# One decoder layer on one Trainium2 core: scores moved beside the values of the head in front, 512-column matmuls first in each such place

## The chip, the core and the metric

The kernel runs on one core of one Trainium2 chip. The metric is the device time of one execution in microseconds (us), the median over the runs shown. An engine is one of PE (TensorE, matmuls; its weight loads are listed apart as PEld), DVE (VectorE), ACT (ScalarE), POOL (GpSimd, here mostly a queue that issues DMAs) and SP (the queue that issues the weight loads from memory). Each engine works through its own list of instructions in the order in which the built program has them; semaphores make one engine wait for another.

## What is computed

One layer of a decoder over 256 tokens and 2048 features: sixteen heads of latent attention beside a short gated convolution, both projected, gated, added, and projected once more. Cut to what matters here:

```python
h = _rmsnorm(x, pre_norm_g)
proj = einsum('bsd,de->bse', h, w_in)          # q_a, c_kv, k_rope, z_mla, c_in, b_gate, c_gate, z_conv, g_mla, g_conv
q  = einsum('bsr,re->bse', _rmsnorm(q_a, q_a_norm_g), w_q_b)     # 16 heads x (128 + 64)
kv = einsum('bsr,re->bse', _rmsnorm(c_kv, kv_a_norm_g), w_kv_b)  # 16 heads x (128 keys + 128 values)
sc = (einsum('bqhd,bkhd->bhqk', q_nope, k_nope) + einsum('bqhr,bkr->bhqk', q_rope, k_rope)) * scale
p  = softmax(where(mask, sc, -inf))
attn = einsum('bhqk,bkhd->bqhd', p, v) * silu(z_mla)
y_mla = attn @ w_o_mla
y_conv = (b_gate * conv(c_gate * c_in) * silu(z_conv)) @ w_o_conv
out = (sigmoid(g_mla) * y_mla + sigmoid(g_conv) * y_conv) @ w_out
x = x + _rmsnorm(out, post_norm_g)
```

## The kernel before

**Numbers in two parts.** Every matmul operand is split into a high part (the value rounded to the matmul's format) and a low part (the rest), and a product is made of three matmuls (`product`, lines 227 to 232). A weight half of 128 x 1024 is split by `split_act` (lines 242 to 249): ACT copies it into a `whi` buffer (line 243), DVE subtracts to give `wlo` (line 244). There are five buffers of each kind; a buffer is free when PE has done its last matmul with it. `ahead` and `take` (lines 202 to 222) load three weight units ahead and split one unit ahead. The same two lines also split other things: `pt` is the split of a head's turned probabilities, `qn_hi`/`qn_lo`, `kn` and `qr` are the splits of queries and keys.

**The middle part** (lines 779 to 858; roughly from 70 to 590 us of the span) is a loop over the sixteen heads h, with v, at = divmod(h, 4). It mixes two kinds of work on PE. The big kind is `channels(h, i)`, i = 0 to 3, and, at every fourth head, `gates(v, i)`: a quarter each, 24 matmuls of 512 columns into two PSUM banks (`quarter`, lines 670 to 676). Between the quarters stand the small steps of attention:

- `group_a(g)`: queries qn and keys kn of two heads. `narrow` and `halves` (lines 234 to 240, 546 to 555) do 8 matmuls of 512 columns for qn, then 8 of 256, evict both banks (`whole`, lines 390 to 394: ACT copies one half out, DVE adds the other) and split; then the same for kn.
- `group_r(g)`: the rotary queries qr, 4 matmuls of 512 and 4 of 256 columns.
- `group_v(v)`: the values of four heads, 24 matmuls of 512 columns.
- `scores(h)`: 8 matmuls, seven of 256 columns and one of 128, then the softmax on DVE and ACT; the exponentials are at line 630. `turned` transposes p on DVE into `via` and POOL sends it to memory in four DMAs (go, line 326); come (line 330) brings it back as p.
- `turn(p)`: splits it into pt (lines 642 to 647); its two instructions are kept in program order.
- `values(h, pt)`: one matmul of 512 columns, then 256, 128 and 256, then `whole` and a product with the gates.

In the version before, the score of head h stands before `channels(h, 0)` (line 812); pt of head h-1 is made after `channels(h, 1)`; values of head h-1 follow `channels(h, 2)` (line 832), with group_a or group_r behind them (`made`, lines 118 to 122: qr at even heads, qn and kn at odd ones, each for the next pair). Where at = 0 and v > 0, the four quarters of the gates come first; pt is made after the second of them and values(h-1) and group_v stand after the third (lines 794 to 799).

**What sets the order.** PE's order is written out: every matmul is kept in program order. On ACT and DVE most instructions are placed by the scheduler that builds the program; a few are kept in order. ACT needs a table in place for some functions: sigmoids (lines 686, 721) and exponentials (line 630) use different ones, and the build puts a table load where the function changes.

Of the kernel before, what the change touches and what calls it, by code (L numbers as in the profile page):

```python
# [12 lines left out]
F32R = mybir.dt.float32r  # L13
# [5 lines left out]
P = 128  # L19
# [63 lines left out]
def tile_layer(ctx: ExitStack, tc: tile.TileContext, xw, w0, xb, x, pos, pvec, post_g, wc, wz, wcv, wkr, wqk, wqr, wv, cwr, wsq, out):  # L83
    nc = tc.nc

    def matmul(*a, **kw):

        return tc.keep_in_program_order(nc.tensor.matmul(*a, **kw))  # L88
# [113 lines left out]
    def ahead(i, raw=3, split=1):  # L202
        while done["raw"] < min(i + raw, len(plan)):
            load_raw(done["raw"])
            done["raw"] += 1
        while done["split"] < min(i + 1 + split, len(plan)):
            while done["raw"] <= done["split"]:
                load_raw(done["raw"])
                done["raw"] += 1
            split_unit(done["split"])  # L210
            done["split"] += 1

    def take(i):
        ahead(i)
        parts = splits.pop(i)

        def piece(j, n):
            o = j * n
            h, o = o // HALF, o % HALF
            return parts[h][0][:, o : o + n], parts[h][1][:, o : o + n]  # L220

        return piece
# [8 lines left out]
        matmul(ps, ah, bl, start=False, stop=False)  # L231
        matmul(ps, al, bh, start=False, stop=last)

    def halves(blocks):


        for ps, w, both, first, _ in blocks:
            matmul(ps[:, :], w[0], both, start=first, stop=False)
        for ps, w, both, _, last in blocks:
            matmul(ps[:, :S], w[1], both[:, :S], start=False, stop=last)  # L240

    def split_act(hi, lo, src, keep=False, later=False):
        a = nc.scalar.activation(hi, src, AF.Copy)  # L243
        b = nc.vector.tensor_tensor(lo, src, hi.bitcast(F32), op=ALU.subtract)  # L244
        if keep:

            tc.keep_in_program_order(a)
        if keep or later:
            tc.keep_in_program_order(b)
# [56 lines left out]
    def temp(name, shape=(P, S), dt=F32, bufs=2, tag=None):  # L306

        tag, n = tag or name.rstrip("0123456789_"), shape[-1]
        if n % LINE == 0:
            return bp.tile(list(shape), dt, name=name, tag=tag, bufs=bufs)  # L310
        return bp.tile([P, -(-n // LINE) * LINE], dt, name=name, tag=tag, bufs=bufs)[:, :n]
# [78 lines left out]
    def whole(dst, ps):  # L390

        t = temp("half")
        nc.scalar.activation(t[:, :], ps[:, S:], AF.Copy)
        nc.vector.tensor_tensor(dst, ps[:, :S], t[:, :], op=ALU.add)
# [146 lines left out]
    def pair(name, shape, bufs=1):  # L541
        return [temp(f"{name}_{n}", shape, F32R, bufs, tag=f"{name}_{n}") for n in ("hi", "lo")]

    groups = {}

    def narrow(names, w, j, src, **kw):
        pss = [bank(n, **kw) for n in names]
        halves([
            (ps, w((j + i) * KR + k, P), src[:, k, :], k == 0, k == KR - 1)
            for i, ps in enumerate(pss) for k in range(KR)  # L550
        ])
        for ps in pss:
            f = temp("f")
            whole(f[:, :], ps)
            yield f

    def group_a(g):

        qn, kn = pair("qn", (P, HG, S)), temp("kn", (P, 2, HG, S), F32R, 1)
        w = take(u_grp["a", g])  # L560
        for n, src, hi, lo in (("qn", qa, qn[0], qn[1]), ("kn", ckv, kn[:, 0], kn[:, 1])):
            fs = narrow([f"{n}{g}_{j}" for j in range(HG)], w, HG * (n == "kn"), src)
            if g == 0 and n == "qn":

                fs = list(fs)
                ahead(u_grp["v", 0])
            for j, f in enumerate(fs):
                split_act(hi[:, j, :], lo[:, j, :], f[:, :])
        groups["a", g] = qn, kn

    def group_r(g):

        qr = temp("qr", (P, HG, S), F32R)

        kw = {} if g else {"tag": "cv", "bufs": 2}
        (f,) = narrow([f"qr{g}"], take(u_grp["r", g]), 0, qa, **kw)
        rope(f[:, :], f[:, :])
        for j in range(HG):

            own, other = (slice(DR * i, DR * i + DR) for i in (j, 1 - j))  # L580
            split_act(qr[own, j, :], qr[other, j, :], f[own, :], g == 0)
        groups["r", g] = qr

    def group_v(v):

        vv = pair("vv", (P, NT, HV * DV))
        w = take(u_grp["v", v])
        for t in range(NT):
            ps = bank(f"vv{v}_{t}")
            for k in range(KR):  # L590
                c = [ckv[:, k, o + t * P : o + (t + 1) * P] for o in (0, S)]
                product(ps[:, :], c, w(k, HV * DV), k == 0, k == KR - 1)
            split_act(vv[0][:, t, :], vv[1][:, t, :], ps[:, :], v == 0)
        groups["v", v] = vv

    def make(i, j):
        {"a": group_a, "r": group_r, "v": group_v}[i](j)

    def scores(h):

# [48 lines left out]
    def values(h, pt):  # L649
        vv = groups["v", h // HV]  # L650
        j = h % HV
        o = bank(f"o{h}", tag="o", bufs=1)
        vs = slice(j * DV, (j + 1) * DV)
        both = o[:, :].rearrange("p (i q) -> p i q", i=2)
        mm = matmul
        mm(both, vv[0][:, 0, vs], pt[:, :, :S], start=True, stop=False)
        mm(o[:, :S], vv[1][:, 0, vs], pt[:, 0, :S], start=False, stop=False)
        mm(o[:, P:S], vv[1][:, 1, vs], pt[:, 0, S:], start=False, stop=False)
        mm(both[:, :, P:], vv[0][:, 1, vs], pt[:, :, S:], start=False, stop=True)

        at = at_t[:, h // HV, :, :].rearrange("p t (i k x) -> p t i k x", i=4, k=HV)[:, :, :, j, :]
        f = temp("f")
        whole(f[:, :], o)
        nc.vector.tensor_tensor(at, f[:, :].rearrange("p (t i x) -> p t i x", t=NT, i=4), at, op=ALU.mult)
# [36 lines left out]
    def channels(h, i):  # L701

        if i == 0:
            cv_ps["now"] = [bank(f"cv{h}_{t}", tag="cv", bufs=2) for t in range(NT)]
        quarter(cv_ps["now"], take(u_head[h][i]), i)
        if i == 3:
            channels_done(*divmod(h, 4))
# [71 lines left out]
    for h in range(H):  # L779
        v, at = divmod(h, HV)  # L780

        if at == 0:
            for i in range(4):
                gates(v, i)
                if v == 0 and i == 0:
                    ckv_come()
                elif v == 0 and i == 1:
                    next(table_parts)
                    key_rope()
                elif v == 0 and i == 2:  # L790
                    latent_split("qa", qa, "q_g")
                elif v and i == 0:
                    arrive()
                elif v and i == 1:
                    pt = turn(ps_by_head.pop(h - 1))
                    next(tap)
                elif v and i == 2:
                    values(h - 1, pt)
                    make("v", v)
            if v:  # L800
                next(tap)
            else:
                latent_split("ckv", ckv, "kv_g")
            gates_done(v)
        if h == 0:

            ahead(u_grp["r", 0])
            for i in first:
                make(*i)
            channels(h, 0)  # L810
        if h < H - 1:
            score(h)
        if h:
            channels(h, 0)
        if at == 0:
            coming.append(gates_turn(v, 0))
        channels(h, 1)
        if at == 0:
            arrive()
            coming.append(gates_turn(v, 1))  # L820
        else:
            pt = turn(ps_by_head.pop(h - 1))
        if h == H - 2:
            score(h + 1)

        if at == 2 or h == H - 1:
            next(tap)
        if at and h < H - 1:
            arrive()
        channels(h, 2)  # L830
        if at:
            values(h - 1, pt)
        else:
            arrive()
            if v:
                coming.append(channels_join(v - 1, 0))
        for i in made[h]:
            make(*i)
        if h == H - 1:
            pt = turn(ps_by_head.pop(h))  # L840
        channels(h, 3)
        if at == 2 or h == H - 1:
            next(tap)
        while coming and h < H - 1:
            arrive()
        if h == H - 1:
            values(h, pt)
        if at == 3:
            coming.append(channels_join(v, 1))
        if at == 1:  # L850
            tap = taps(v, 1)
            next(tap)
        elif at == 3 and h + 1 < H or h == H - 2:
            tap = taps(v, 0)
            next(tap)
# [280 lines left out]
```

## Time and profile before

| | |
|---|---|
| median of 3 runs | 1035.66 us (1035.56 to 1035.92) |
| the profiled execution | 1034.93 us, of it the span from its first to its last instruction 1033.2 us |
| PE busy | 1026.7 us, 99% of the span, 4680 matmuls |
| DVE busy | 682.9 us, 66% |
| ACT busy | 526.7 us, 51% |
| granted TensorE clock | 0.999 |
| largest weight loads | 80 + 64 + 16 loads of 1 MB (raw from wsq, wcv and wz) |

The groups of instructions are read as line, engine, operation, tile written <- tiles read, count | busy us, mean ns of one | idle time before them and what ended it. A row of the timeline is: start in us, length in us, engine, line, operation, tiles, shape, count and, in brackets, the idle time before it with what ended it. The stated ends of matmuls are modelled and overlap the next one, so the time a matmul takes in a stream is read from start to start.

### The profile page before, as it was taken

The page shows a single profiled execution, that of the slowest core. Times are in us where ns is not written, and L with a number is a line of the kernel's source. Part 1 is how long each engine was busy: PE and PEld are TensorE (multiplying, and loading weights), DVE is VectorE, ACT ScalarE, POOL GpSimd, SP SyncE. Part 2 cuts the span into 40 slices and gives each one's busy share as a digit, 9 for nine tenths or more (in the row PEclk, how much of TensorE's full clock was granted, in tenths as well). Part 3 has the DMA queues.
Part 4 walks back from the last instruction along what each step waited for, and adds up shares of the span by engine and source line. Part 5 has one row for each costly group of instructions (what it writes and reads, how often), then busy time and mean ns, then how long its engine had stood idle before and what let it go on. Part 6 is the DMA issues. An engine that isn't in the chain of part 4 may idle for free.

```text
span 1033.2 us, 12728 instructions
## 1 busy us (share of the span) xinstructions
PE 1026.7 (99%) x4680; PEld 855.0 (83%) x4680; DVE 682.9 (66%) x957; ACT 526.7 (51%) x734; POOL 179.8 (17%) x344
## 2 busy tenths in 40 slices
PE   9999999999999999999999999999999999999997
PEld 7888888888888888888888888888888888888886
DVE  7588777777787777767767785564455455455562
ACT  7766545555455454564555565344434444443551
POOL 4640421104201142112413120020010001002000
PEclk9999999999999999999999999999999999999999
DMA  9775766568565775856766765565565556558642
GB/s 359 281 252 215 267 236 215 204 220 284 194 254 186 232 283 187 278 179 244 264 236 225 258 222 201 204 223 190 199 217 208 189 202 242 180 189 336 230 167 81
DMA packets 44670, 233.25 MB, mean 226 GB/s; under 512 B 7968, under 2 KB 10656, under 8 KB 21696
## 3 DMA queue, kind: packets, MB, share of 16 engines
q1 hardware_dynamic: 32544, 199.67, 54.2%
q0 software_dynamic: 11632, 29.48, 8.8%
q10 hardware_dynamic: 432, 3.29, 0.8%
q8 instruction: 36, 0.59, 0.2%
q14 instruction: 26, 0.21, 0.1%
HBM read 215.66 MB, written 12.58 MB: 221 GB/s over the span
## 4 chain that ended last, share of the span: by engine, by line
PE 99%; DVE 0%; ACT 0%; issue 0%
PE cv L88 34%; PE sq L88 34%; PE out L88 8%; PE z L88 8%; PE qa L88 2%; PE qn L88 2%; PE kn L88 2%; PE vv L88 2%; PE ckv L88 2%; PE sc L88 1%; PE qr L88 1%; PE o L88 1%; PE idle L88 0%; PE kr L88 0%; DVE og L989 0%; ACT junk L970 0%
## 5 line engine op out<-in xcount | busy, mean ns | idle before, releaser
L244 DVE TENSOR_TENSOR wlo<-raw,whi 128x1024 fp32r<-128x1024 f32 (+1 forms) x370 | 440.4, 1197 | 284.2 <-ACT whi L243 273.5
L243 ACT ACTIVATE whi<-raw 128x1024 fp32r<-128x1024 f32 (+1 forms) x372 | 382.5, 1035 | 402.5 <-PE sq L88 180.5
L88 PE MATMUL cv<-whi,x_both 128*128 128x512 f32 x1024 | 321.1, 389 | 0.0
L88 PEld LDWEIGHTS cv<-whi,x_both 128*128 128x128 f32 x1024 | 192.3, 188 | 39.2
L88 PE MATMUL cv<-wlo,x_both 128*128 128x512 f32 x512 | 199.5, 390 | 0.0
L88 PE MATMUL sq<-whi,x_both 128*128 128x512 f32 x512 | 158.2, 389 | 0.0
L88 PEld LDWEIGHTS sq<-whi,x_both 128*128 128x128 f32 x512 | 96.1, 188 | 19.9
L88 PEld LDWEIGHTS cv<-wlo,x_both 128*128 128x128 f32 x512 | 96.2, 188 | 19.0
L88 PE MATMUL sq<-wlo,x_both 128*128 128x512 f32 x256 | 99.6, 389 | 0.0
L88 PE MATMUL z<-whi,x_both 128*128 128x512 f32 x256 | 80.0, 389 | 0.0
L88 PE MATMUL sq<-whi,at_both 128*128 128x512 f32 x256 | 79.4, 389 | 0.0
L88 PE MATMUL sq<-whi,cv_both 128*128 128x512 f32 x256 | 79.4, 389 | 0.0
L88 PE MATMUL out<-whi,m_both 128*128 128x512 f32 x256 | 79.0, 389 | 0.0
L326 POOL DMA_DIRECT2D far<-sg x32 | 17.5, 552 | 311.7 <-DVE sg L318 238.3
L326 POOL DMA_DIRECT2D far<-via x64 | 35.2, 557 | 183.8 <-DVE via L318 183.8
L88 PEld LDWEIGHTS out<-whi,m_both 128*128 128x128 f32 x256 | 48.0, 188 | 10.0
L88 PEld LDWEIGHTS sq<-wlo,x_both 128*128 128x128 f32 x256 | 48.0, 188 | 10.0
L88 PEld LDWEIGHTS z<-whi,x_both 128*128 128x128 f32 x256 | 48.0, 188 | 10.0
L88 PEld LDWEIGHTS sq<-whi,cv_both 128*128 128x128 f32 x256 | 48.0, 188 | 9.9
L88 PEld LDWEIGHTS sq<-whi,at_both 128*128 128x128 f32 x256 | 48.0, 188 | 9.9
L88 PE MATMUL z<-wlo,x_both 128*128 128x512 f32 x128 | 49.8, 389 | 0.0
L88 PE MATMUL sq<-wlo,at_both 128*128 128x512 f32 x128 | 49.8, 389 | 0.0
(216 smaller groups left out, 1126.2 us busy)
## 6 DMA issues: line engine op xcount, KB each, us to landing
raw<-wsq_dram SPq DMA_DIRECT2D x80, 1024.0 KB, 4.8
raw<-wcv_dram SPq DMA_DIRECT2D x64, 1024.0 KB, 5.6
raw<-wz_dram SPq DMA_DIRECT2D x16, 1024.0 KB, 4.9
raw<-wqk_dram SPq DMA_DIRECT2D x8, 1024.0 KB, 5.7
cw<-cwr_dram POOLq DMA_DIRECT2D x24, 256.0 KB, 5.8
raw<-wc_dram SPq DMA_DIRECT2D x4, 1024.0 KB, 9.9
raw<-wv_dram SPq DMA_DIRECT2D x4, 1024.0 KB, 5.4
far<-via POOLq DMA_DIRECT2D x64, 48.0 KB, 3.5
```

Source lines behind the costliest of these rows:

```text
L88: return tc.keep_in_program_order(nc.tensor.matmul(*a, **kw))
L243: a = nc.scalar.activation(hi, src, AF.Copy)
L244: b = nc.vector.tensor_tensor(lo, src, hi.bitcast(F32), op=ALU.subtract)
L326: tc.keep_in_program_order(queue.dma_start(out=f[i], in_=m))
```

## The change

PE's order is changed around the small steps. `halves` is cut into `first_parts` (the 512-column matmuls) and `second_parts` (the 256-column ones); `narrow` does the first and returns a function for the rest; `group_a`, `group_r`, `group_v` and `values` become generators that stop after their 512-column matmuls. `group_a` can do those of qn and kn together.

- Odd heads up to 13 (at = 1 or 3; seven heads): the score of h no longer stands before `channels(h, 0)` but between `channels(h, 2)` and `channels(h, 3)`, after the 512-column matmuls of group_a and of values(h-1) and before all the narrower ones. Where at = 3, qn and kn go together; where at = 1, kn's matmuls follow at the end as before.
- Heads 4, 8 and 12 (at = 0): the score of h moves forward to the third quarter of the gates, between the first matmul of values(h-1) and its other three.
- Heads 2, 6, 10, 14 (at = 2) and 0 keep their score before `channels(h, 0)` or next to it; values and qr there are merged in the same way, 512 columns first. Head 15 keeps its place.
- The `arrive` calls that issue the way back of p (come) move with the scores.

```diff
-    def halves(blocks):
+    def first_parts(blocks):
         for ps, w, both, first, _ in blocks:
             matmul(ps[:, :], w[0], both, start=first, stop=False)
+
+    def second_parts(blocks):
         for ps, w, both, _, last in blocks:
             matmul(ps[:, :S], w[1], both[:, :S], start=False, stop=last)
...
     def narrow(names, w, j, src, **kw):
         pss = [bank(n, **kw) for n in names]
-        halves([
+        blocks = [
             (ps, w((j + i) * KR + k, P), src[:, k, :], k == 0, k == KR - 1)
             for i, ps in enumerate(pss) for k in range(KR)
-        ])
-        for ps in pss:
-            f = temp("f")
-            whole(f[:, :], ps)
-            yield f
+        ]
+        first_parts(blocks)
+
+        def rest():
+            second_parts(blocks)
+            for ps in pss:
+                f = temp("f")
+                whole(f[:, :], ps)
+                yield f
+
+        return rest
...
+    def group_a(g, together=False):
+        w = take(u_grp["a", g])
+        q = narrow([f"qn{g}_{j}" for j in range(HG)], w, 0, qa)
+        keys = lambda: narrow([f"kn{g}_{j}" for j in range(HG)], w, HG, ckv)
+        k = keys() if together else None
+        yield
...
+        for j, f in enumerate((k or keys())()):
+            split_act(kn[:, 0, j, :], kn[:, 1, j, :], f[:, :])
...
+    def finish_all(*steps):
+        for g in steps:
+            for _ in g:
+                pass
...
         mm(both, vv[0][:, 0, vs], pt[:, :, :S], start=True, stop=False)
+        yield
         mm(o[:, :S], vv[1][:, 0, vs], pt[:, 0, :S], start=False, stop=False)
...
                 elif v and i == 2:
-                    values(h - 1, pt)
-                    make("v", v)
+                    o = values(h - 1, pt)
+                    next(o)
+                    score(h)
+                    finish_all(o, make("v", v))
...
             gates_done(v)
+            if v:
+                arrive()
...
-        if h < H - 1:
+        if at == 2:
+
             score(h)
-        if h:
-            channels(h, 0)
+        channels(h, 0)
+        if h == 0:
+            score(h)
...
-        if at and h < H - 1:
+        if at == 2:
             arrive()
         channels(h, 2)
+
+
+        steps = [make(*i, *([at == 3] if i[0] == "a" else [])) for i in made[h]]
         if at:
-            values(h - 1, pt)
-        else:
+            steps.append(values(h - 1, pt))
+        for g in steps:
+            next(g)
+        if at in (1, 3) and h < H - 1:
+            score(h)
+        if not at:
             arrive()
             if v:
                 coming.append(channels_join(v - 1, 0))
-        for i in made[h]:
-            make(*i)
+        finish_all(*steps[::-1])
```

The counts of matmuls, of DVE instructions and of DMAs are the same in both built programs. ACT's list has 12 table loads before and 24 after.

More of the change, by code (lines that the diff above doesn't have):

```diff
@@ L547, in narrow @@
         pss = [bank(n, **kw) for n in names]
-        halves([
+        blocks = [
             (ps, w((j + i) * KR + k, P), src[:, k, :], k == 0, k == KR - 1)
             for i, ps in enumerate(pss) for k in range(KR)
-        ])
-        for ps in pss:
-            f = temp("f")
-            whole(f[:, :], ps)
-            yield f
-    def group_a(g):
-        qn, kn = pair("qn", (P, HG, S)), temp("kn", (P, 2, HG, S), F32R, 1)
[L560 to L568, printed above, removed]
+        ]
[13 more added lines that the diff above has]
+        yield
+        qn, kn = pair("qn", (P, HG, S)), temp("kn", (P, 2, HG, S), F32R, 1)
+        fs = q()
+        if g == 0:
+            fs = list(fs)
+            ahead(u_grp["v", 0])
+        for j, f in enumerate(fs):
+            split_act(qn[0][:, j, :], qn[1][:, j, :], f[:, :])
+        for j, f in enumerate((k or keys())()):
+            split_act(kn[:, 0, j, :], kn[:, 1, j, :], f[:, :])
         groups["a", g] = qn, kn
     def group_r(g):
+        kw = {} if g else {"tag": "cv", "bufs": 2}
+        rest = narrow([f"qr{g}"], take(u_grp["r", g]), 0, qa, **kw)
+        yield
         qr = temp("qr", (P, HG, S), F32R)
-        kw = {} if g else {"tag": "cv", "bufs": 2}
-        (f,) = narrow([f"qr{g}"], take(u_grp["r", g]), 0, qa, **kw)
+        (f,) = rest()
         rope(f[:, :], f[:, :])
@@ L594, in group_v, with make @@
         groups["v", v] = vv
-    def make(i, j):
-        {"a": group_a, "r": group_r, "v": group_v}[i](j)
+        yield
+    def make(i, j, *more):
+        return {"a": group_a, "r": group_r, "v": group_v}[i](j, *more)
+    def finish_all(*steps):
+        for g in steps:
+            for _ in g:
+                pass
     def scores(h):
@@ L656, in values @@
         mm(both, vv[0][:, 0, vs], pt[:, :, :S], start=True, stop=False)
+        yield
         mm(o[:, :S], vv[1][:, 0, vs], pt[:, 0, :S], start=False, stop=False)
@@ L808, in tile_layer @@
             for i in first:
-                make(*i)
-            channels(h, 0)
-        if h < H - 1:
+                finish_all(make(*i))
+        if at == 2:
             score(h)
-        if h:
-            channels(h, 0)
+        channels(h, 0)
+        if h == 0:
+            score(h)
         if at == 0:
@@ L836, in tile_layer @@
                 coming.append(channels_join(v - 1, 0))
-        for i in made[h]:
-            make(*i)
+        finish_all(*steps[::-1])
         if h == H - 1:
@@ L846, in tile_layer @@
         if h == H - 1:
-            values(h, pt)
+            finish_all(values(h, pt))
         if at == 3:
```

## The prediction

> **What bounds the kernel now.** I read the page's busy times first, then PE's list of waits, then the timeline of PE, ACT and DVE at two places the change touches, last the chain of work that ended last.
>
> ```profile
> span 1033.2 us, 12728 instructions
> PE 1026.7 (99%) x4680; PEld 855.0 (83%) x4680; DVE 682.9 (66%) x957; ACT 526.7 (51%) x734; POOL 179.8 (17%) x344
> PE 99%; DVE 0%; ACT 0%; issue 0%
> ...
> PE fin L88 <- ACT dg L1011: 0.9, 1, 0.9
> ```
>
> PE is the chain, and it waits for another engine once, 0.9 us at the very end (the list has one more entry, PE's own start). Whatever is won must come out of the matmul stream itself; whatever makes PE wait in the middle is added to the end in full. PE's timeline, at the third gate quarter of heads 3/4 and at head 5:
>
> ```profile
> 192.97 0.39 PE L88 MATMUL z<-whi,x_both 128*128 128x512 f32 x1
> ...
> 209.29 0.39 PE L88 MATMUL o<-pt,vv_hi 128*128 128x512 f32 x1
> ...
> 262.21 0.39 PE L88 MATMUL o<-pt,vv_hi 128*128 128x512 f32 x1
> ...
> 262.78 2.01 PE L88 MATMUL qn<-qa,whi 128*128 128x512 f32 x8
> 264.63 1.11 PE L88 MATMUL qn<-qa,wlo 128*128 128x256 f32 x8
> 265.58 2.00 PE L88 MATMUL kn<-ckv,whi 128*128 128x512 f32 x8
> 267.42 1.11 PE L88 MATMUL kn<-ckv,wlo 128*128 128x256 f32 x8
> 268.37 0.40 PE L88 MATMUL cv<-whi,x_both 128*128 128x512 f32 x1
> ...
> 273.83 0.28 PE L88 MATMUL sc<-kn,qn_hi 128*128 128x256 f32 x1
> ...
> 274.77 0.39 PE L88 MATMUL cv<-whi,x_both 128*128 128x512 f32 x1
> ```
>
> From 192.97 to 209.29 stand three quarters, 72 matmuls: 0.2267 us for 512 columns undisturbed, 0.1133 for 256. Eight of 512 should take 1.81 and eight of 256 0.91; the rows have 1.85 and 0.95 (qn), 1.84 and 0.95 (kn). The quarter from 268.37 to 273.83 takes 5.46 against 24 x 0.2267 = 5.44. So a narrow matmul costs some 0.005 us over its columns, and the 512-column ones right after a narrow stretch 0.03 us in all.
>
> **What grouping saves.** It removes ends of narrow stretches: two at each of heads 1, 5, 9, 13 (score and values no longer end in 512-column work), three at 3, 7, 11, one each at 2, 6, 10 and one at each of the three gate places: 8 + 9 + 3 + 3 = 23. At 0.03 us that is 0.7 us; about 0.2 goes back, since the first narrow matmul of a stretch, now joined, loses its free start (0.005 to 0.01 us, 23 times). Taken: -0.5 us. From both sides: 0, and -5 us if every narrow matmul also fell to its columns. That bound is head 5's own excess, 268.37 - 262.21 = 6.16 for 13440 columns that need 5.95, plus 0.94 - 0.85 for the score, 0.3 us, times 16 heads. I am near the first, since the narrow matmuls stay as many.
>
> **First cost: pt at the three gate places (values of heads 3, 7, 11).** The score of these heads moves back by three quarters, so p comes back later, and the build has moved the split into pt on ACT and DVE. Built order on ACT after the change, head 7 (four neighbours in the list, same at 3 and 11):
>
> ```
> whi(unit 69, half 2) <- raw
> whi(unit 70, half 1) <- raw     waits for PE: last matmul of gate quarter 3 (unit 67)
> pt <- p
> sc_half <- sc8
> ```
>
> DVE has wlo(unit 70, half 1) ahead of its pt too. The halves share five buffers, and unit 70's first takes that of unit 67's second. But PE's next matmul after that quarter is the values' first, which waits for pt. So the weight split starts only when PE has finished, and PE stands until both splits are through. Before, pt stood two quarters ahead (198.22, behind a split freed early); the late weight split at 209.50 held up nobody:
>
> ```profile
> 198.22 0.51 ACT L243 ACTIVATE pt<-p 128x384 fp32r<-128x384 f32 x1
> ...
> 209.50 1.06 ACT L243 ACTIVATE whi<-raw 128x1024 fp32r<-128x1024 f32 x1 [0.30 <-PE z L88]
> 210.47 0.36 ACT L393 ACTIVATE half<-o 128x256 f32<-128x256 f32 x1
> ...
> 275.57 1.22 DVE L244 TENSOR_TENSOR wlo<-raw,whi 128x1024 fp32r<-128x1024 f32 x1
> 276.71 0.28 DVE L619 TENSOR_TENSOR p<-sc,sc_half 128x128 f32<-128x128 f32 x1
> ...
> 281.69 0.55 DVE L244 TENSOR_TENSOR pt<-p,pt 128x384 fp32r<-128x384 f32 x1
> ```
>
> With E the time at which values would start (209.29 there): whi starts at E + 0.21 and ends at E + 1.27; pt's ACT part (0.51) runs from E + 1.18 (209.50 to 210.47) to 1.69; DVE's wlo starts at E + 1.30, the next instruction 1.14 later (275.57 to 276.71), so pt's DVE part runs from E + 2.44 to 2.99. PE goes on at E + 3.0. From both sides: nothing if p's split got ahead, 3.2 with full lengths in place of start to start. Taken: 3 x 3.0 = 9.0 us. Behind the waiting matmul stand score h+1, the values of four heads, the fourth quarter; nothing more is late, as their weights were split before. The way of p is hidden: transposed, it needs four issues, landing and the way back,
>
> ```profile
> L326 POOL DMA_DIRECT2D far<-via x64 | 35.2, 557 | 183.8 <-DVE via L318 183.8
> far<-via POOLq DMA_DIRECT2D x64, 48.0 KB, 3.5
> p<-far POOLq DMA_DIRECT2D x16, 192.0 KB, 4.2
> ```
>
> 4 x 0.56 + 3.5 + 4.2 = 9.9 us, and from the end of the score to E there are 2.3 us of narrow matmuls and four quarters, 24 us.
>
> **Second cost: keys at heads 5, 9, 13.** There the score of h now stands at the place that makes the next pair's qn and kn, and the score of h+1 follows one quarter later. Its softmax is in the same ACT and DVE lists, ahead of the split of kn. Also the function changes more often (the 12 new table loads), and at these heads a load is the instruction before the exponentials. Rows for the walk:
>
> ```profile
> 267.62 1.06 ACT L243 ACTIVATE whi<-raw 128x1024 fp32r<-128x1024 f32 x1 [1.18 <-PE kn L88]
> 268.58 0.40 ACT L243 ACTIVATE qn_hi<-f 128x256 fp32r<-128x256 f32 x1
> 268.89 0.36 ACT L393 ACTIVATE half<-kn 128x256 f32<-128x256 f32 x1
> ...
> 228.05 1.28 ACT L630 ACT_TABLE_LOAD   x1
> 229.34 0.40 ACT L630 ACTIVATE p<-p,nb 128x128 f32<-128x128 f32 x1
> ...
> 271.40 0.74 DVE L716 SCALAR_TENSOR_TENSOR cv_f<-cv,r_both,cv_f 128x512 f32<-128x512 f32 x1
> 272.06 0.75 DVE L244 TENSOR_TENSOR kn<-f,kn 128x256 fp32r<-128x256 f32 x2
> ...
> 278.28 0.40 ACT L630 ACTIVATE p<-p,nb 128x128 f32<-128x128 f32 x1 [3.02 <-DVE nb L627]
> ...
> 279.17 1.05 ACT L243 ACTIVATE whi<-raw 128x1024 fp32r<-128x1024 f32 x1
> ...
> 279.30 0.17 DVE L634 RECIPROCAL rs<-sm 128x2 f32<-128x2 f32 x1 [1.05 <-ACT p L630]
> 279.50 0.55 DVE L637 TENSOR_SCALAR p<-p,rs 128x128 f32<-128x128 f32 x2
> 280.08 0.58 DVE L318 STREAM_TRANSPOSE via<-p 128x384 f32<-128x384 f32 x1
> 280.59 1.18 DVE L244 TENSOR_TENSOR wlo<-raw,whi 128x1024 fp32r<-128x1024 f32 x1
> ```
>
> Count T from the place's first matmul. Nine of 512 (2.04), score (0.94), values' rest (262.78 - 262.21 less one of 512, 0.34), qn narrow (0.95), kn wide (1.84) and narrow (0.95) end at 7.06; with the quarter (5.46) the next score is due at T = 12.5. ACT's weight split waits for kn's last wide matmul (6.11) and starts 0.21 later, 6.32. Then qn_hi at 7.28 (+0.96), half of kn at 7.59 (+0.31), the load at 7.90 (+0.31), exponentials at 9.19 (+1.29), the second qn_hi at 10.08 (+0.89), done at 10.49. DVE's list from there is qn_lo (0.33, as one of the pair at 272.06), f of kn (0.33), two scalings of p (0.58), the other f (0.33), eviction of cv (0.66), transpose (0.51), first kn part (0.42): 10.5 + 3.16 = 13.7. Late by 1.2 us; in the trace before the same split was done at 272.48, 1.35 ahead of 273.83. Head 1 has this order without the load, 1.29 earlier: 12.4, just in time. From both sides: 0 if DVE runs closer, 2.0 with full lengths in place of start to start. Taken: 3 x 1.2 = 3.6 us. Where it comes, the next score and the quarter behind it are late together, and nothing else.
>
> [...]
>
> **Edits costed at nothing.** The other nine table loads, 1.28 us each, fall where ACT's splits wait for PE to free a buffer; from the freeing of one of the five buffers to the use of the half split into it PE has over a quarter of other matmuls (5.4 us). Head starts without a score lose 0.94 us in which the cv banks were emptied:
>
> ```profile
> 298.76 0.69 ACT L718 ACTIVATE cv_w<-cv,r_both 128x512 f32<-128x512 f32 x1 [0.30 <-PE cv L88]
> ```
>
> ACT waits for the bank's last matmul and empties it in 0.69; it is needed half a quarter (2.7) later. Uncovered, each would cost its lateness.
>
> **Sum.** 9.0 + 3.6 - 0.5 = +12.1. The profiled execution took 1034.93 (span 1033.2 and 1.7 around it), so 1047.0; the median of the runs is 0.73 above the profiled one, so 1047.8.
>
> **Rivals.**
> - *Only pt stalls.* kn's split was 1.35 early before and my walk lives on sums of tenths. 1035.66 + 9.0 - 0.5 = 1044.2. Chance 0.17.
> - *The clock falls in the stalls.* Granted clock after the last matmul, which ends at 1028.35 (first row, of PE's timeline):
>
> ```profile
> 1027.22 1.13 PE L88 MATMUL fin<-og,dg 128*128 128x256 f32 x4 [0.87 <-ACT dg L1011]
> ...
> 1030.40:1031.40 1.00, 0.00 (x0) 0.00 (x0) 0.00 (x0) 0.00 (x0) 0.00 (x0) 1.00 0.85 303
> 1031.80:1032.20 0.40, 0.00 (x0) 0.00 (x0) 0.00 (x0) 0.00 (x0) 0.00 (x0) 0.50 0.00 0
> ```
>
>   It halves between 3.1 and 3.5 us of rest. A stall of 3.0 is just below. If it does, and as long again passes at half speed, each costs 1.7 more: 1052.9. Chance 0.10. [...]
> - *ACT is held longer at the new loads.* If the exponentials start later by as much again as a load lasts (1.28), kn costs 3 x (1.2 + 1.28) = 7.4: 1051.6. Against it: 229.34. Chance 0.05. [...]
> - *Not slower: pt's split isn't held.* It decides at each gate place: from the point where the weight buffer comes free 3.0 us ahead of E, nothing waits, kn's lateness apart. Speaks against: the same split waited for PE's z at 209.50 before. If kn is in time as well, 1035.66 - 0.5 = 1035.2, no change; with the bound of the savings 1030.7. Chance 0.04 and 0.02.
> - The forecast has the remaining 0.62.
>
> **How the numbers follow.** The forecast's own range is 1045 to 1050. To leave out no more than 2 in 10 it has to reach down to pt alone (1044.2, or 1043 with cheaper stalls) and up to the dearer stalls (1052.9): 1043 to 1053. A measurement of this kernel tells some 0.2% (2 us) from no change. Faster by more: 0.02; within: 0.04; slower: 0.94.
>
> **What would show it.** PE's waits, empty before, should list o <- DVE pt three times, some 3.0 us each, near 210, 350 and 485, with ACT's pt row behind a whi released by PE z; and sc <- DVE kn three times, about 1 us, at heads 6, 10 and 14. Table loads should be 24. After a score in a merged place no 512-column matmul should follow. I am wrong if PE's waits stay empty, if pt stands ahead of that whi, or if the clock leaves 1.00 in the middle.

## The result, and the profile after

The changed kernel took 1053.83 us (1052.48 to 1054.63, 4 runs), the kernel before, beside it, 1035.72 us (1035.56 to 1035.92): a ratio of 1.0175, 95% interval 1.0158 to 1.0191. It is 18.1 us slower, where 12.1 were forecast; the time lies 0.8 us above the forecast range. The profiled execution is the longest of the four, 1054.63 us, and stands 19.7 us above the profiled execution before (1034.93).

The page of the changed kernel, then its list of PE's waits (engine, tile, line <- what it waited for: us in all, times, longest):

```profile
span 1052.9 us, 12732 instructions
PE 1034.1 (98%) x4680; PEld 860.3 (82%) x4680; DVE 679.2 (65%) x957; ACT 547.3 (52%) x746; POOL 178.8 (17%) x344
```

```profile
PE o L88 <- DVE pt L246: 8.9, 3, 3.0
PE sc L88 <- DVE kn L246: 3.1, 3, 1.0
...
PE vv L88 <- DVE f L396: 0.3, 1, 0.3
```

Two groups are new in the middle of the kernel: three waits for pt of 3.0 us, three for kn of 1.0. But 8.9 + 3.1 is only 12 of 19.7 us, and PE's busy time has grown too, from 1026.7 to 1034.1 us for the same 4680 matmuls. Waiting can't do that; slower matmuls can. The second of the three gate places, in the timeline:

```profile
350.28 0.39 PE L88 MATMUL z<-whi,x_both 128*128 128x512 f32 x1
350.44 2.58 DVE L246 TENSOR_TENSOR wlo<-raw,whi 128x1024 fp32r<-128x1024 f32 x2 [2.68 <-ACT whi L245]
350.70 1.06 ACT L245 ACTIVATE whi<-raw 128x1024 fp32r<-128x1024 f32 x1 [0.30 <-PE z L88]
351.67 0.51 ACT L245 ACTIVATE pt<-p 128x384 fp32r<-128x384 f32 x1
...
352.94 0.55 DVE L246 TENSOR_TENSOR pt<-p,pt 128x384 fp32r<-128x384 f32 x1
...
353.63 0.76 PE L88 MATMUL o<-pt,vv_hi 128*128 128x512 f32 x1 [2.97 <-DVE pt L246]
```

Read from the top: PE's last matmul of the third gate quarter, the weight split on ACT released by it, pt on ACT behind that, DVE's two wlo and its pt, and only then PE's values. From 350.28 to 353.63 are 3.35 us where a 512-column matmul takes 0.23: 3.12 us lost. The last row holds a second thing: this matmul lasts 0.76 us, where an undisturbed one of its kind lasts 0.39. The granted clock (last but two of the numbers) around the three places; columns are the window, its length, PE's busy time (instructions), granted clock, DMA share, GB/s:

```profile
213.40:213.60 0.20, 0.20 (x1) 0.74 0.95 266
213.60:216.80 3.20, 3.20 (x14) 0.50 0.99 335
216.80:217.00 0.20, 0.20 (x2) 0.72 0.58 246
353.40:353.60 0.20, 0.00 (x0) 0.61 1.00 277
353.60:356.80 3.20, 3.17 (x13) 0.50 1.03 312
356.80:357.00 0.20, 0.20 (x2) 0.86 0.80 328
493.20:493.40 0.20, 0.00 (x0) 0.97 1.31 348
493.40:500.20 6.80, 6.31 (x20) 0.50 0.86 281
500.20:500.40 0.20, 0.20 (x2) 0.96 0.00 0
```

The clock is at 0.50 behind each of the three. The rows at the edges give the moments: a mean of 0.74 over 213.40 to 213.60 means full speed for 48% of it, so it fell at 213.50 and, likewise, rose at 216.91: 3.42 us. At the second place it is 353.44 to 356.86, 3.41 us; at the third 493.39 to 500.22, 6.83 us, twice that. At 0.50 a matmul of 512 columns takes 0.425 us from start to start (four from 496.80 to 498.50) in place of 0.227. From the values' first matmul to one of the next group (vv) behind the rise the change takes 4.30 us (213.31 to 217.61), 4.23 (353.63 to 357.86) and 7.02 (493.89 to 500.91); pt_half, below, with the clock at 1.00, takes 2.74, 2.74 and 4.10 for the same matmuls. So 1.6, 1.5 and 2.9 us are lost, 6.0 us in all.

Behind the late keys the clock stays (1.00 over 276 to 286, 416 to 426 and 558 to 568). The timeline of ACT, DVE and PE at head 5:

```profile
274.81 1.28 ACT L653 ACT_TABLE_LOAD   x1
...
277.13 0.17 DVE L657 RECIPROCAL rs<-sm 128x2 f32<-128x2 f32 x1 [1.30 <-ACT p L653]
...
279.17 0.39 PE L88 MATMUL cv<-whi,x_both 128*128 128x512 f32 x1
...
280.06 0.72 DVE L246 TENSOR_TENSOR kn<-f,kn 128x256 fp32r<-128x256 f32 x2
...
280.58 0.36 PE L88 MATMUL sc<-kn,qn_hi 128*128 128x256 f32 x1 [1.03 <-DVE kn L246]
```

The load holds the exponentials, DVE waits 1.30 us for them, kn comes last, and the next score starts 1.41 us after the matmul before it, 1.18 more than undisturbed.

### The profile page after: what moved, and what is told of

Same layout as the page of the kernel before. It is cut to its first block, busy times and chain, and to the rows that moved or that the text cites. A ratio compares the mean times of both kernels' runs of the same rounds, so it can differ in the third digit from the quotient of the medians.

```text
span 1052.9 us, 12732 instructions
## 1 busy us (share of the span) xinstructions
PE 1034.1 (98%) x4680; PEld 860.3 (82%) x4680; DVE 679.2 (65%) x957; ACT 547.3 (52%) x746; POOL 178.8 (17%) x344
## 4 chain that ended last, share of the span: by engine, by line
PE 93%; DMA 2%; ACT 2%; DVE 2%; issue 1%; DVEq 0%; SPq 0%
PE sq L88 33%; PE cv L88 32%; PE out L88 8%; PE z L88 6%; PE vv L88 2%; PE qa L88 2%; PE kn L88 2%; PE qn L88 2%; PE ckv L88 2%; PE sc L88 2%; PE o L88 1%; PE qr L88 1%; DMA raw<-wz_dram 1%; DMA at_f<-far_qa 1%; ACT whi L245 1%
```

## The experiments

All ran beside the kernel before, whose medians in these three groups were 1035.21, 1035.73 and 1035.59 us, with single runs from 1034.78 to 1037.39; the last run had 1035.67. So less than half a microsecond isn't told apart by a median here.

### Take pt out from behind the weight splits (pt_ahead)

```diff
+    pt_first = [u for v in range(1, NV) for u in (u_gate[v][3], u_head[HV * v][0])]
...
-            split_act(hi[:, :n], lo[:, :n], t[:, h : h + n], i == u_head[0][1], i in (u_grp["r", 0], ...))
+            split_act(hi[:, :n], lo[:, :n], t[:, h : h + n], i == u_head[0][1] or i in pt_first, i in (...))
```

Those splits are now kept in program order, in which pt comes first.

> The split of pt is put ahead of the splits of the fourth gate quarter's and the next head's first weights on ACT and DVE at the three gate places; nothing else is changed. Theory (pt stands behind a weight split that waits for PE, and the pause lets the clock fall): all three pauses of 3.13 us and the stretches at half clock (1.6, 1.6 and 3.1 us) go, so 1053.8 - 9.4 - 6.3 = 1038.1, between 1037.5 and 1039.5, granted clock 1.00 in the middle, no o <- DVE pt among PE's waits, and sc <- DVE kn stays at three times 1.0. Rival A (the clock falls for another reason at these places, for example the narrow score put there): the clock still goes to 0.50 there and the time is 1043 to 1045. Rival B (the two weight splits, now behind pt and the first evictions of score and values, come too late for the fourth gate quarter): z <- DVE wlo or ACT whi appears among the waits and some 1 to 3 us a place come back, 1041 to 1047.

Measured: 1040.07 us (1039.84 to 1042.69), ratio 1.0050 (1.0037 to 1.0063). All three waits for pt are gone, those for kn are as they were. The time is 0.6 above the theory's range, and rival B was partly right. DVE, then PE, in the profiled execution, the longest of the four:

```profile
356.80 0.69 DVE L781 TENSOR_TENSOR mv<-mv,cw 128x512 f32<-128x512 f32 x1 [3.27 <-DMA cw<-cwr_dram]
...
359.13 2.36 DVE L247 TENSOR_TENSOR wlo<-raw,whi 128x1024 fp32r<-128x1024 f32 x2
...
360.40 0.80 PE L88 MATMUL cv<-wlo,x_both 128*128 128x512 f32 x1 [2.18 <-DVE wlo L247]
```

Kept in order, the weight splits stand behind a step of the convolution that waits for a transfer (cw), and where that one is late PE waits 2.18 us for wlo. This is a cost of the edit, not of the change. It shows one thing more: the matmul behind this pause lasts 0.80 us. The clock halved there too, though no score stands at that place:

```profile
356.80:360.20 3.40, 1.42 (x7) 1.00 0.49 198
360.20:360.40 0.20, 0.00 (x0) 0.66 0.00 0
360.40:363.60 3.20, 3.20 (x8) 0.50 0.29 79
363.60:363.80 0.20, 0.20 (x2) 0.80 0.54 149
```

Fallen at 360.26, risen at 363.68: 3.42 us again, after 2.0 us of rest. Rival A falls.

### Fill the pause (fill8)

```diff
+                    fill = bank(f"fill{v}", tag="st", bufs=1)
+                    for _ in range(8):
+                        matmul(fill[:, :], x_both[:, 0, :P], x_both[:, 0, :], start=True, stop=True)
                     o = values(h - 1, pt)
```

> The change as it is, with eight matmuls of 512 columns more (their result is not used) between the third gate quarter and the first matmul of values at each of the three places. They take 1.81 us of the pause and pt's way is as before, so the values start at the same time. Theory (the pause itself lets the clock fall): PE's idle time there goes from 3.0 to 1.2 us, the clock stays at 1.00, and 6.3 us of half clock go: 1047.5, between 1046.8 and 1048.5. Rival A (the clock falls for another reason at these places): time and clock as with the change, 1052.5 to 1054.6. Rival B (the eight make pt later in some way): above 1053, with a longer o <- DVE pt.

Measured: 1049.28 us (1048.36 to 1051.24), ratio 1.0135 (1.0122 to 1.0148). PE's wait for pt, and the clock over each place (pause and what follows):

```profile
PE o L88 <- DVE pt L246: 3.5, 3, 1.2
```

```profile
209.00:218.00 9.00, 7.84 (x40) 1.00 0.99 324
348.00:357.00 9.00, 7.84 (x40) 1.00 0.95 305
487.00:496.00 9.00, 7.84 (x41) 1.00 1.01 343
```

pt is as late as before (8 x 0.227 of matmuls and 1.2 us of waiting), the clock stays at 1.00 at all three, and the kernel is 4.6 us faster for 24 more matmuls (4.0 if each is taken against the kernel before that ran beside it). So the half clock came with the rest, not with what stands there. The time is 0.8 over the expected range: that was formed from the median of the change less the 6.3 us put down to the clock in its longest execution, and the shorter ones have a higher mean clock (1052.48 one of 0.995, 1054.63 one of 0.992).

### Half the delay (pt_half)

Only the later of the two weight splits is put behind pt, on ACT alone:

```diff
+    pt_first = [u_head[HV * v][0] for v in range(1, NV)]
...
-        if keep:
+        if keep or hi_only:
             tc.keep_in_program_order(a)
```

> Of the two weight splits that stand ahead of pt at the three gate places, only the one that waits for PE's last matmul of the third gate quarter is put behind pt (on ACT); the one of the fourth quarter's second half stays ahead. It waits for the last use of the third quarter's first half, six matmuls (1.36 us) ahead of that quarter's end, so the same walk of splits ends 1.36 us earlier: a pause of 3.13 - 1.36 = 1.8 us instead of 3.13. Theory (how much of a stretch of 3.4 us is rest decides the clock; 2.2 us of rest were enough in the pt_ahead run, 1.0 to 1.2 were not): 3 x 1.36 = 4.1 us less pause for certain, and half clock after none to two of the three places: 1044 to 1048, with o <- DVE pt at 1.6 each. Rival A (any pause of over 1.5 us is followed by half clock): half clock after all three, 1048 to 1050. Rival B (pt waits for something else than the chain of splits): pauses of 3.0 as before.

Measured: 1044.28 us (1043.48 to 1045.10), ratio 1.0081 (1.0067 to 1.0094). PE's wait for pt, and the clock over the three places:

```profile
PE o L88 <- DVE pt L247: 4.8, 3, 1.6
```

```profile
209.00:218.00 9.00, 7.39 (x39) 1.00 0.97 326
346.00:355.00 9.00, 7.39 (x38) 1.00 0.99 334
483.00:492.00 9.00, 7.39 (x38) 1.00 1.00 330
```

The values wait 1.61 us in place of 2.97; with the 0.15 that the loss was over the wait before (3.12), 1.76 us a place, where 1.8 was expected. Of the 9.5 us that are saved the shorter pauses are 3 x 1.36 = 4.1, the clock, now at 1.00, is the rest.

### Cut the pause in two (mid2)

```diff
+                    fill = bank(f"fill{v}", tag="st", bufs=1)
+                    ahead(u_gate[v][3])
+                    for _ in range(2):
+                        matmul(fill[:, :], splits[u_head[h][0]][0][0][:, :P], x_both[:, 0, :], start=True, stop=True)
                     o = values(h - 1, pt)
```

> The change as it is, with two matmuls of 512 columns (0.45 us, result not used) at each of the three gate places that start when ACT has split the first half of the next head's first weights, that is in the middle of the pause. The pause of 3.13 us is cut into two of about 1.3 and 1.2 us; pt comes as before. Theory (the share of rest in a stretch of fixed length decides): 2.5 us of rest in some 3.1 us are still more than the 2.1 that were followed by half clock, so time and clock stay near the change's own: 1051.5 to 1054.5, 0.50 granted after at least two places. Rival (the length of one unbroken rest decides, between 1.3 and 2.2 us): the clock stays at 1.00 and the time is that of fill8, 1048 to 1049.5.

Measured: 1053.61 us (1050.40 to 1054.73), ratio 1.0166 (1.0152 to 1.0180). Waits, then the clock at the first place (two rows), at the second (three) and at the third (two):

```profile
PE fill L88 <- ACT whi L245: 3.4, 3, 1.1
PE o L88 <- DVE pt L246: 3.3, 3, 1.1
```

```profile
208.00:211.40 3.40, 2.25 (x10) 1.00 0.91 312
211.40:214.80 3.40, 2.31 (x15) 1.00 1.07 318
...
348.00:351.40 3.40, 1.53 (x6) 1.00 1.03 342
351.40:351.60 0.20, 0.00 (x0) 0.61 0.94 225
351.60:354.60 3.00, 2.84 (x12) 0.50 1.00 232
...
487.98:491.39 3.41, 1.74 (x7) 1.00 1.01 363
491.40:498.20 6.80, 6.25 (x20) 0.50 0.88 293
```

No single rest is longer than 1.15 us, shorter than in pt_half (1.61), and yet the clock halves at two places of three. So the length of one rest doesn't tell these cases apart; the rest in the 3.4 us that end where the clock falls goes with it: 1.9 us at the second place (3.40 - 1.53) and 1.67 us at the third (3.41 - 1.74). At the first place an edge, counted back from the second (211.49, an estimate, see the last section), lies in the same pause; the rows beside it have 1.15 and 1.09 us of rest, and the clock stays at 1.00.

### Load the exponential's table early (load_early)

```diff
+        if at == 1 and v:
+            tc.keep_in_program_order(
+                nc.scalar.activation(temp("warm", (P, NT), bufs=1)[:, :1], r_col[:, 0:1], AF.Exp))
         channels(h, 1)
```

> The change as it is, with one exponential of a single column more (result not used) at the start of heads 5, 9 and 13, so that the table of the exponential is loaded there and not between the splits of the keys. Built order of everything else at these places is the same. Theory (the late load makes kn late by its 1.28 us): kn comes 1.28 us earlier, late by 1.2 - 1.28, so the three waits sc <- DVE kn go and 3 x 1.27 = 3.8 us are saved: 1050.0 (1048.7 to 1050.8). Rival (the softmax and the evictions in DVE's list ahead of kn are what is late, the load is hidden behind them): less than 1.2 us saved in all, above 1052, sc <- DVE kn stays at 0.7 or more.

Measured: 1052.11 us (1050.53 to 1052.90), ratio 1.0163 (1.0148 to 1.0177). All three waits for kn are gone, as the theory says; the time is 1.3 us over its range. In this execution the clock fell at two of the three pauses. At the first, PE's pause of 2.97 us (values at 213.50) lies across 211.8, which is an edge by the same count (211.78):

```profile
208.40:211.80 3.40, 2.13 (x10) 1.00 0.85 316
211.80:215.20 3.40, 1.70 (x13) 1.00 1.08 336
...
351.60:351.80 0.20, 0.00 (x0) 0.83 1.01 277
```

Rest of 1.27 and 1.70 us on the two sides, and full clock; the last row is the edge at which it fell behind the second pause. So 1.70 us in one piece passed here where 1.67 us in two pieces did not in mid2. Rest is counted from the modelled ends of matmuls, which lie some 0.16 us behind the start of the next one in a stream (0.39 long, 0.227 from start to start); counted from start to start, mid2's two pauses have 2.0 us in that stretch, and this one 1.7. The runs tell it no finer than that.

By the time alone the rival (above 1052) came out as well; the waits decide against it. The profiled execution is the shortest of the four, with a mean clock of 0.996; the others have 0.992 to 0.994. What the edit itself cost is shown by third_back_load below.

### Both repairs (both_fixed)

The edits of pt_ahead and load_early together.

> The edits of pt_ahead and load_early together: the order of the matmuls is the change's, the two causes of waiting are gone. Theory (those two causes and the clock are all that the change costs, but for 0.6 us of waits at head 0): before - 0.5 for the grouped narrow stretches + 0.6 at head 0 = 1035.8, between 1035.3 and 1036.3, PE's waits empty in heads 1 to 15. Rival A (grouping saves more than 0.5 and this was covered by the stalls): under 1035.0. Rival B (something else of the change still costs, head starts without a score or the other table loads): over 1037.

Measured: 1039.70 us (1038.01 to 1044.26), ratio 1.0050 (1.0033 to 1.0068). A miss by 3.9 us, on the side of rival B. Neither kn nor pt is among PE's waits, but `cv <- DVE wlo` is (0.9 us in the profiled execution), as in pt_ahead. The two edits bring costs of their own, so this run says nothing of the rest of the change. The next four do without them.

### The grouping alone, and with three scores moved (grouped_only, grouped_gate)

```diff
-                    next(o)
-                    score(h)
-                    finish_all(o, make("v", v))
+                    finish_all(values(h - 1, pt), make("v", v))
...
+        if h < H - 1:
             score(h)
...
-        if at in (1, 3) and h < H - 1:
-            score(h)
```

grouped_gate leaves the first of these parts as the change has it, so that the scores of heads 4, 8 and 12 stand at the gate place.

> The grouping alone: matmuls of 512 columns first, then the narrow ones, in the places that make queries, keys, rotary parts and take values; all sixteen scores stay where they stood before the change. Theory (grouping saves 0.03 us an end of a narrow stretch, and everything that was lost came with the moved scores): some 14 ends, 0.4 us less 0.1 given back, 0.3 us faster than before, ratio 0.9995 to 1.0000; PE's waits empty in heads 1 to 15, 12 table loads. Rival A (grouping is worth nothing or costs buffers): 1.0000 to 1.0010. Rival B (narrow matmuls also fall to their columns): over 1 us faster, under 0.9990.

> As grouped_only, and the scores of heads 4, 8 and 12 also at the gate place behind the values' first matmul, as in the change; the scores of all other heads stay where they stood. So the score of head 3 is early, and only its neighbour is moved. Theory (pt is late because the score of heads 3, 7, 11 was moved back, not because a score stands behind it): no o <- DVE pt among PE's waits, clock 1.00, within 0.5 us of grouped_only. Rival A (the score at the gate place itself makes the pause): three pauses, 1045 to 1053. Rival B (the six table loads more that this order has hold a split): some waits z or cv <- DVE wlo, 1 to 3 us.

Measured: 1035.59 us (1034.79 to 1036.72), ratio 1.0000 (0.9991 to 1.0009), and 1034.76 us (1034.26 to 1036.09), ratio 0.9992 (0.9983 to 1.0000). Neither has a wait in the middle; of grouped_gate:

```profile
PE fin L88 <- ACT dg L1044: 0.9, 1, 0.9
PE idle L88 <- PEq L1157: 0.8, 1, 0.8
PE qa L88 <- ACT whi L245: 0.2, 1, 0.2
```

A score behind the values' first matmul makes no pause. Whether the grouping alone wins its 0.3 us stays below what the runs resolve. grouped_gate was run once more:

> The kernel of grouped_gate again, beside other runs of the kernel before. If its 1034.76 us against 1035.73 was its own, the ratio is again 0.9985 to 0.9997 (0.3 to 1.5 us faster); by the narrow ends that it removes only 0.4 to 0.5 us are explained, so a ratio of 0.9995 is the likeliest; if it was the day's spread, 0.9998 to 1.0005.

Measured: 1034.93 us (1034.39 to 1035.33), ratio 0.9994 (0.9985 to 1.0002).

### Three of the ten moves undone (third_back)

```diff
-        if at == 2:
+        if at == 2 or at == 3 and h < H - 1:
             score(h)
...
-        if at in (1, 3) and h < H - 1:
+        if at == 1:
             score(h)
```

> The change, but the scores of heads 3, 7 and 11 (the last of four heads) stand at the head's start again, as before the change; all else as in the change. Theory (pt is late only because these three scores were moved back three quarters; its pauses and the half clock that they bring are 9.4 + 4.7 to 6.3 us of the change's 18, the keys 3.8): no o <- DVE pt, clock 1.00 in the middle, sc <- DVE kn three times 1.0, so before + 3.8 - 0.5 = 1039.0, between 1038.4 and 1039.6. Rival A (the keys are late because of the pauses ahead of them, or the other way round): the waits of kn go too, 1035 to 1036. Rival B (other moved parts cost as well): over 1040.

Measured: 1038.27 us (1038.07 to 1038.78), ratio 1.0028 (1.0018 to 1.0039).

```profile
PE sc L88 <- DVE kn L246: 3.1, 3, 1.0
```

Three scores moved back to the head's start take 15.6 of the change's 18.1 us away: the pauses for pt, their half clock, and the scatter between executions with it (0.7 us in place of 2.2). The keys wait as before, so the two causes are independent.

### The keys repaired in two ways (third_back_load, third_back_load2)

The first adds load_early's edit to third_back. The second takes another tile and another place:

```diff
             pt = turn(ps_by_head.pop(h - 1))
+        if at == 1 and v:
+            tc.keep_in_program_order(nc.scalar.activation(warm[:, :], mhalf[:, :], AF.Exp))
```

> As third_back, and the exponential's table loaded early at heads 5, 9 and 13 as in load_early: seven of the ten scores moved, all the grouping, neither of the two causes. Theory: 0.4 to 0.9 us faster than before, ratio 0.9990 to 1.0000, PE's waits empty in heads 1 to 15; at most 0.3 us from grouped_gate. Rival (the early load, 1.28 us of ACT between two weight splits, or the head starts without a score delay a channel's eviction): cv <- ACT cv_f of 0.2 to 0.4 us at heads 5, 9 and 13, no faster than before.

> As third_back_load, with the exponential of one column written to a tile that the kernel has already (so every other tile stays at its address) and put behind pt on ACT, where ACT then waits 3 us for PE. In third_back_load the three waits of kn went (4.0 us), but 1.1 us of cv <- ACT cv_f and 1.5 to 1.9 us of narrow and values' matmuls a few ns longer came. Theory (the place of the load held the eviction, the added tile moved the addresses of the others): both costs go, 1038.27 - 4.0 = 1034.3, between 1034.0 and 1035.0, ratio 0.9987 to 0.9996. Rival (the early load costs the same wherever it stands, or the narrow matmuls lengthen for another reason): 1036 to 1037.5.

Measured: 1037.94 us (1037.16 to 1038.48), ratio 1.0023 (1.0013 to 1.0032), and 1034.78 us (1034.12 to 1035.53), ratio 0.9992 (0.9983 to 1.0001). In the first, ACT does the load (245.42 to 246.70) ahead of an eviction that PE's next channel waits for (it starts at 247.69, in third_back at 245.63). The lateness is too short to stand in PE's list of waits; it shows in the spacing of the channel's matmuls, where one pair takes 0.94 us in place of 0.62. And the values' matmuls differ, here as groups (min/median/max in ns) without and with the edit:

```profile
L88 PE MATMUL vv<-whi,ckv x64: 387/389/397, 81.0 to 487.2; 128*128 128x512 f32 x64
```

```profile
L88 PE MATMUL vv<-whi,ckv x64: 388/393/404, 80.9 to 487.0; 128*128 128x512 f32 x64
```

The waits for kn go, but the eviction comes late and the values' matmuls last some 4 ns longer; most of the gain is eaten. With an old tile and a place where ACT would wait for PE the time is 3.2 us lower and PE's busy time 1025.8 us in place of 1028.8, and of PE's waits only the two of the kernel before are left (fin, 0.9 us, and idle, 0.8).

This version has all the grouping and seven of the ten moves. At 1034.78 us it and grouped_gate are the fastest of the study, 0.7 to 0.9 us under the kernel before (grouped_gate's two runs, and this one). The intervals reach 1, so that they are faster isn't shown.

## Why the prediction was wrong

The direction held, and so did the mechanisms of the two costs; the size was 6.0 us short, and most of that is one step, on the clock.

**The step that failed: "It halves between 3.1 and 3.5 us of rest. A stall of 3.0 is just below."** The end of the kernel showed one pause and one fall of the clock, and I read from it a limit on the length of a rest. What the runs showed in its place: the clock fell and rose at points whole stretches of 3.41 us apart, and its falls went with the rest within the stretch in front. 2.0 us (pt_ahead) and 1.9 and 1.67 us in two pieces (mid2) were followed by half clock; 1.70 us (load_early) and 1.6 us (pt_half) in one piece were not. A pause of 3.0 us is above all of these; one such pause, with an edge near its middle by that count (load_early, 1.27 and 1.70), was not followed by half clock, all others were. The sum had the clock at nothing; it cost 6.0 us in the profiled execution, and by the medians some 4 to 4.6 us (fill8) or 9.5 - 4.1 = 5.4 us (pt_half). That the clock leaves 1.00 in the middle was the prediction's own sign of being wrong. The rival that had it ("The clock falls in the stalls", each 1.7 more, 1052.9) came close for two places (1.6 and 1.5) but not for the third (2.9), and stood at a chance of 0.10. That as long again passes at half speed was my estimate; the runs showed 3.42 and 3.41 us, and 6.83 at the third place.

**First cost, 3 x 3.0.** 3 x 3.12 measured; places, order and releaser are as walked. pt_half confirms the walk from the other side (1.8 expected, 1.76 measured), third_back that the score's move is its reason.

**Second cost, 3 x 1.2.** 3 x 1.18, and the load is its cause: loaded early, the waits vanish. Head 1 was to be just in time and shows no wait.

**What grouping saves, -0.5.** Not separable by medians. PE's busy time, 1026.7 us before, is 1026.5 in grouped_only and 1025.8 in third_back_load2, 0.2 and 0.9 less; but the spans of grouped_gate's two profiled executions, one kernel, are 1033.0 and 1032.6, so this doesn't settle it either. The -0.5 stays an estimate.

**Edits costed at nothing.** The other table loads and the head starts without a score cost nothing that PE's waits show; third_back_load2, with six of the twelve new loads and the head starts of seven of the ten moved scores, waits nowhere in the middle. Where a load did cost, at heads 5, 9 and 13, it stands under the second cost.

**Head 0.** From the first qn matmul to the first channel's take 13.33 us in the profiled execution (73.85 to 87.18) and 12.45 before, 0.9 us more, of which the list above shows 0.3 (vv <- DVE f). PE's order there is that of before, and third_back, with the same order there, has no such wait in its list; load_early has it (0.3). A transfer that ACT waits for there (ckv) came 1.2 us later in this execution, at 70.91 in place of 69.73. So it looks like this execution's and not the change's; the cause isn't shown.

**The sum, for the profiled execution:** 9.4 (pt) + 3.5 (kn) + 6.0 (clock) - 0.5 (grouping) = 18.4 of 19.7 us, with the grouping as estimated; with the 0.9 us of head 0 some 0.4 are left that aren't placed.

## What to carry to other kernels

Price a pause on PE by its length and by the granted clock behind it. Here a pause of 1.6 us (pt_half) cost its length; with 1.9 us of rest or more in the 3.4 us that end at the fall it cost some 1.5 us more (1.6 and 1.5 in the change, 1.4 in mid2), and near 1.7 us both were seen. At two places (the third of the change and of mid2) it was 2.9 more. Breaking it up didn't help (mid2, 1053.61 against 1053.83 us) while filling it did (fill8, 1049.28). When a step is moved so that it becomes ready later, look at which work the build now places ahead of it, and above all whether that work waits for the very engine that the step feeds. A repair is an edit as well: a kept order brought a wait of 2.18 us here (pt_ahead), an added tile and the place of a table load 3.2 us together (third_back_load), before the right form gave the whole gain.

## What the runs showed of the hardware

**The clock's changes were whole stretches apart.** In the profiled execution of the change the clock fell at 213.50, 353.44 and 493.39: 139.95 us apart, 41 times 3.413, where the clock stayed at 0.50 for 3.42, 3.41 and 6.83 us. It fell once more behind the last matmul, at 1049.76 (0.91 over 1049.60 to 1049.80), 549.54 us or 161 times 3.413 behind the last rise. In load_early it fell at 351.73 (0.83 over 351.60 to 351.80) and at 491.68 (0.70 over 491.60 to 491.80), in mid2 at 351.44 and 491.39, each time 139.95 us apart again. The edges in front are counted from this, as an estimate: 139.95 before 351.73 is 211.78, inside load_early's first pause, which it cuts into 1.27 and 1.70, and before 351.44 it is 211.49, inside mid2's first. In pt_half the clock was at 1.00 at all three places. Its three pauses are 137.40 us apart (values at 211.75, 349.15 and 486.55), 40.25 times 3.413, so that, by the same estimate, an edge can't cut both the first and the third of them: one of the two had its 1.61 us of rest in one stretch, at full clock. Whether the edges lie elsewhere in each execution isn't shown, as one execution of each run was profiled; the mean clocks of mid2's four are 0.992 to 0.998.

**The clock came back behind less rest than it fell behind.** At the third place of the change the stretch from 493.39 held only 0.5 us of rest, and the clock stayed at 0.50 for a second one, as it did at mid2's third place with 0.55 (6.80 - 6.25); behind 0.2 us of rest at the change's second place, and 0.3 at mid2's, it rose. So in these traces it returned behind a stretch with up to 0.3 us of rest and not behind one with 0.5, while near 1.7 us it was seen both to fall and to stay. The end of the kernel, from which the prediction read, shows the fall alone.

**The values' matmuls were longer in the three runs with an added tile.** Their medians are 393, 394 and 393 ns in load_early, both_fixed and third_back_load, each with one small tile added, and 389 in the kernel before, the change, pt_ahead, fill8, pt_half, mid2 and third_back. Whether the tile, the addresses of the others or the early load is the reason, and what of the 3.2 us is theirs, wasn't tried by itself.
